# Decoder trunk on one core: values as stationary weights, key blocks merged by the mask, gelu in one function, last sums earlier

## The chip, the cores and the metric

The kernel runs on one core of a Trainium2 chip. A time is the device time of one execution in microseconds (us), and a kernel's time is the median of its runs. TensorE is called PE here, VectorE DVE, ScalarE ACT, GpSimd POOL and SyncE SP, as the profile does; PEld is PE's loading of stationary weights.

## The reference

Two layers work on 256 positions of width 2048 in float32. What matters here:

```python
for l in range(2):
    h = rms_norm(x, mix_norm[l])
    q, k, v, uv, gate_logits = split(h @ w_in[l])      # 1024, 256, 256, 2048, 4096 columns
    q, k = rope(rms_norm(q)), rope(rms_norm(k))        # 16 query heads, 4 key heads of 64
    # query i sees the 128 keys i-127 .. i; one learned sink for each head joins the softmax
    branch_a = softmax(q k^T / 8, window, sink) @ v @ w_attn_branch[l]
    u, v2 = split(gelu(uv))                            # the tanh form of gelu
    branch_b = (u * (tril(W_s) @ layer_norm(v2) + b)) @ w_sgu_branch[l]
    g = sigmoid(gate_logits)
    x = x + (g[:, :2048] * branch_a + g[:, 2048:] * branch_b) @ w_out[l]
    h2 = rms_norm(x, ffn_norm[l])
    x = x + (silu(h2 @ w_gate[l]) * (h2 @ w_up[l])) @ w_down[l]   # width 5632
```

## The kernel before

**The weight stream.** The positions are two tiles of 128 rows, t = 0 and 1. A weight matrix is cut into chunks of 512 columns, and a chunk into raw tiles of 256 rows (128 partitions x 2 x 512, 512 KB). Each raw tile is one entry of a list that is fixed before the program is written. SP loads it (L218). ACT rounds it to a high part `whi` (L244), and DVE subtracts that to give the low part `wlo` (L245). The activations are held in the same way as `uh` and `ul`. `add_product` then makes three matmuls of 128x512 for each of 2 x 128 rows (L340, L341): high by high, low by high, high by low. An ordinary entry multiplies both position tiles, so it is 12 matmuls.

Where two chunks are multiplied by the same activations (`product_pair`), a part of them goes through a scheme of seven products instead of eight. Its entries (tags P1 to P7) have 6 matmuls each; DVE makes differences of raw tiles for them (L229), and of the activations: `sums` (L499), rounded to `sh` by ACT (L484) and `sl` by DVE (L485). After P5, ACT copies one accumulator into `kept` (L363) and moves another into its place (L364), and P6 adds to the accumulator that has been read.

`whi` and `wlo` have four buffers each. The stream loads 7 entries ahead and splits 4 ahead, so ACT can start a `whi` when PE has ended the entry four places earlier.

**What sets the order.** PE's instructions stand in the order in which the program is written. All other work hangs on a count of ticks. `step()` writes one entry; two products make a tick, so an ordinary entry is one tick and a 6-matmul entry half of one. `after(n, fn)` puts `fn` n ticks ahead, and `tick()` writes what is due. On ACT, DVE and POOL a scheduler orders the instructions at build time; SP and POOL also hold queues from which transfers start.

**Attention.** For position tile t and key head g (4 query heads), `scores` multiplies queries by all keys of one or two blocks (`psc`, L754; 128 keys at t = 0, 256 at t = 1), adds a mask on DVE (L758), takes maximum, exponentials and sums. Five ticks later `weights` transposes the 128x128 blocks on PE (`ppt`, L783): 4 at t = 0 and 8 at t = 1. Three ticks later `values` multiplies them by v (`po`, L793), with the transposed probabilities as the stationary operand and 64 columns of v as the moving one, and DVE divides by the sum (L797). For each c, a half of the query heads, the result `att` is transposed (`transposed`, L410) by DVE and by 16 small transfers on SP's queue (L416).

**Spatial gating.** `half` brings chunks of u and v out of PSUM, halved; `gelu` then takes a square and a tanh on ACT and two products on DVE for each of eight 128x512 tiles in a layer. `center`, `scaled` and `shifted` normalize v, `mix` multiplies it by the spatial matrix `wsT` (`psg`, L871). The spatial matrix is transposed on PE 40 ticks after the layer's start (`pw`, L653) into two PSUM tiles that `ppt` uses too, and DVE copies it out (L654).

**The feed-forward stage** runs in rounds of 4, 4 and 3 chunks. The activations of a round's first chunk (`hid`) get their sums at the ticks of `WINO_HID`, and the down projection needs them.

## Time and profile before

| | |
|---|---|
| median of 3 runs | 2461.22 us (2460.16 to 2461.9) |
| profiled execution, its own time | 2457.45 us |
| its span, first to last instruction | 2455.7 us |
| PE busy | 2438.1 us (99%) |
| DVE busy | 1999.5 us (81%) |
| ACT busy | 1472.5 us (60%) |
| POOL busy | 315.6 us (13%) |
| matmuls of L340 and L341 | 10398 |

A busy share is a mean over the stages. PE's matmuls are pipelined: each shows some 0.39 us, but one starts every 0.23 us, so what a matmul costs is read from the distance between starts and not from its length. In the rows, `out<-in` names the tiles, then come the shapes and the count.

### The profile page before, as it was taken

Reading aid. Unit: us, or ns where it says so; the run is one execution under the profiler, and the core shown is the slowest. Engines: PE = TensorE matmul, PEld = TensorE weight load, DVE = VectorE, ACT = ScalarE, POOL = GpSimd, SP = SyncE. Lnnn points to the kernel's source line nnn. Section 1 sums busy time; section 2 is a strip of 40 time slices with the busy share of each in tenths; the row PEclk is TensorE's granted clock in tenths of the full one; section 3 lists DMA queues with packets and bytes.
Section 4 is the critical chain, followed back from the end, with each engine's and each line's share of the span. In section 5 each row is a group of like instructions: output and inputs, shape, how many; then the busy total and the mean of one; then the engine's idle time right before and its main releaser. Section 6 shows DMA issues by size and latency. Waiting matters only on the chain.

```text
span 2455.7 us, 31363 instructions
## 1 busy us (share of the span) xinstructions
PE 2438.1 (99%) x10968; PEld 2012.6 (82%) x10968; DVE 1999.5 (81%) x2320; ACT 1472.5 (60%) x1842; POOL 315.6 (13%) x592
## 2 busy tenths in 40 slices
PE   9999999999999999999999999999999999999999
PEld 7888888888888888887887888888888888888877
DVE  6798676797978997899877986768878789978996
ACT  5567544576655665566655665545666556655664
POOL 3100002132210111001101000021322101110110
PEclk9999999999999999999999999999999999999999
DMA  9555657576667657665747446675767675667654
GB/s 299 196 187 163 212 198 220 186 236 210 220 217 233 210 176 231 230 203 170 229 155 257 152 157 223 202 215 177 246 202 236 204 245 189 200 209 241 203 179 139
DMA packets 280782, 506.74 MB, mean 206 GB/s; under 512 B 28272, under 2 KB 40144, under 8 KB 280624
## 3 DMA queue, kind: packets, MB, share of 16 engines
q1 hardware_dynamic: 262544, 486.35, 61.0%
q0 software_dynamic: 17760, 18.12, 2.8%
q8 instruction: 86, 1.41, 0.2%
q14 instruction: 72, 0.59, 0.1%
q10 hardware_dynamic: 320, 0.27, 0.0%
HBM read 475.27 MB, written 2.10 MB: 194 GB/s over the span
## 4 chain that ended last, share of the span: by engine, by line
PE 90%; DVE 3%; DMA 3%; SPq 1%; issue 1%; ACT 1%; DVEq 0%; ACTq 0%
PE acc L340 59%; PE acc L341 29%; DMA raw<-in_w_in_dram 2%; DVE wlo L245 2%; SPq L416 1%; ACT whi L244 1%; PE po L793 1%; PE psc L754 0%; PE ppt L783 0%; DVE raw L229 0%; PE psg L871 0%; PE pt L453 0%; DMA raw<-in_w_up_dram 0%; DMA raw<-in_w_down_dram 0%; DVE box L410 0%
## 5 line engine op out<-in xcount | busy, mean ns | idle before, releaser
L244 ACT ACTIVATE whi<-raw 128x1024 fp32r<-128x1024 f32 (+1 forms) x1074 | 1132.0, 1059 | 883.0 <-PE acc L341 623.4
L245 DVE TENSOR_TENSOR wlo<-raw,whi 128x1024 fp32r<-128x1024 f32 (+1 forms) x1075 | 1301.3, 1219 | 399.0 <-ACT whi L244 386.7
L340 PE MATMUL acc<-whi,uh 128*128 128x512 f32 x2994 | 1170.3, 391 | 1.2 <-ACT uh L439 1.2
L340 PE MATMUL acc<-wlo,uh 128*128 128x512 f32 x2994 | 1167.1, 390 | 3.0 <-DVE wlo L245 2.9
L341 PE MATMUL acc<-whi,ul 128*128 128x512 f32 x2994 | 1166.4, 390 | 0.0
L340 PEld LDWEIGHTS acc<-wlo,uh 128*128 128x128 f32 x2994 | 562.6, 188 | 123.2 <-DVE wlo L245 6.0
L340 PEld LDWEIGHTS acc<-whi,uh 128*128 128x128 f32 x2994 | 562.6, 188 | 117.7 <-ACT uh L439 1.4
L341 PEld LDWEIGHTS acc<-whi,ul 128*128 128x128 f32 x2994 | 562.3, 188 | 117.8 <-DVE ul L444 0.5
L416 POOL DMA_DIRECT2D tt<-box x544 | 266.5, 497 | 1697.0 <-ACT whi L244 695.5
L229 DVE TENSOR_TENSOR raw<-raw,raw 128x1024 f32<-128x1024 f32 x236 | 287.8, 1219 | 1.6 <-DMA raw<-in_w_up_dram 0.8
L341 PE MATMUL acc<-whi,sl 128*128 128x512 f32 x472 | 184.0, 390 | 3.2 <-DVE sl L485 3.2
L340 PE MATMUL acc<-whi,sh 128*128 128x512 f32 x472 | 184.8, 392 | 1.7 <-ACT acc L364 1.7
L340 PE MATMUL acc<-wlo,sh 128*128 128x512 f32 x472 | 184.2, 390 | 0.0
L341 PEld LDWEIGHTS acc<-whi,sl 128*128 128x128 f32 x472 | 88.6, 188 | 22.5 <-DVE sl L485 4.0
L340 PEld LDWEIGHTS acc<-whi,sh 128*128 128x128 f32 x472 | 88.6, 188 | 20.9 <-ACT acc L364 2.1
L340 PEld LDWEIGHTS acc<-wlo,sh 128*128 128x128 f32 x472 | 88.7, 188 | 18.0
L366 DVE TENSOR_TENSOR kept<-acc,kept 128x512 f32<-128x512 f32 x94 | 64.3, 684 | 10.1 <-PE acc L341 10.1
L369 ACT ACTIVATE acc<-kept 128x512 f32<-128x512 f32 x94 | 54.9, 586 | 4.3 <-DVE kept L366 4.2
L888 DVE SCALAR_TENSOR_TENSOR xs<-acc,xs 128x512 f32<-128x512 f32 (+1 forms) x66 | 42.0, 668 | 8.4 <-PE acc L341 8.1
L436 DVE TENSOR_TENSOR ul<-tt,uh 128x512 fp32r<-128x512 f32 x52 | 34.0, 684 | 2.9 <-ACT uh L435 2.9
L435 ACT ACTIVATE uh<-tt 128x512 fp32r<-128x512 f32 x52 | 29.8, 618 | 9.4 <-DMA tt<-box 9.4
L312 POOL TENSOR_TENSOR rv<-ve,neg_half 128x4 f32<-128x4 f32 x8 | 11.9, 1486 | 172.9 <-DVE ve L839 159.5
(137 smaller groups left out, 874.8 us busy)
## 6 DMA issues: line engine op xcount, KB each, us to landing
raw<-in_w_in_dram SPq DMA_DIRECT2D x239, 512.0 KB, 4.7
raw<-in_w_gate_dram SPq DMA_DIRECT2D x176, 512.0 KB, 4.4
raw<-in_w_up_dram SPq DMA_DIRECT2D x176, 512.0 KB, 4.9
raw<-in_w_down_dram SPq DMA_DIRECT2D x176, 512.0 KB, 5.0
raw<-in_w_out_dram SPq DMA_DIRECT2D x64, 512.0 KB, 5.0
tt<-box POOLq DMA_DIRECT2D x544, 32.0 KB, 4.2
raw<-in_w_attn_branch_dram SPq DMA_DIRECT2D x32, 512.0 KB, 5.6
raw<-in_w_sgu_branch_dram SPq DMA_DIRECT2D x32, 512.0 KB, 4.4
```

The source lines that it names most:

```text
L229: self.last = nc.vector.tensor_tensor(out=self.raws[d], in0=self.raws[x], in1=self.raws[y], op=ALU.subtract)
L244: self.high = nc.scalar.activation(hi[:, i, :], raw[:, i, :], AF.Copy)
L245: self.last = nc.vector.tensor_tensor(out=lo[:, i, :], in0=raw[:, i, :], in1=hi[:, i, :].bitcast(F32), op=ALU.subtract)
L340: nc.tensor.matmul(ps, a, part[:, kk, :], start=first and kk + n == 0, stop=False, skip_group_check=True)
L341: nc.tensor.matmul(ps, b, hi[:, kk, :], start=False, stop=kk == 1, skip_group_check=True)
L366: nc.vector.tensor_tensor(out=p.kept[:, int(tag == "P7"), :], in0=a[1], in1=p.kept[:, 1, :], op=ALU.add)
L369: nc.scalar.activation(ps, p.kept[:, t, :], AF.Copy)
L416: q.dma_start(dst[j * B:(j + 1) * B, i], box[i * B:(i + 1) * B, j])
L435: nc.scalar.activation(h, s_, AF.Copy)
L436: nc.vector.tensor_tensor(out=l, in0=s_, in1=h.bitcast(F32), op=ALU.subtract)
L793: nc.tensor.matmul(po[:, h, :], pT[kb][:, h, :], self.kv[:, kb, KVW + g * HD:KVW + (g + 1) * HD], start=kb == 0, stop=kb == t)
L888: nc.vector.scalar_tensor_tensor(out=xs[:, t, sl], in0=sums[t][:, i * w:(i + 1) * w], scalar=scale, in1=xs[:, t, sl], op0=ALU.mult, op1=AL ...
```

## The change

- **Values.** v is now the stationary operand (128 keys x 64 columns) and the transposed probabilities of four heads are the moving one (512 columns). Two key heads write to the two halves of one PSUM tile, partitions 0 to 63 and 64 to 127. The result is already transposed, so `att`, its transposing and its transfers go; ACT and DVE take `uh` and `ul` from it. Heads lie in another order, so the 32 loads of `w_attn_branch` become 64 of half the partitions (`rows_of`). The division by the sum moves to the probabilities ahead of their transposing.
- **Key blocks.** Each query sees 128 of 256 keys: for each key column, one of the two blocks. At t = 1 ACT copies the later block's scores and DVE overwrites those that the mask forbids with the earlier block's (`copy_predicated`). Exponentials, maximum and transposing run over 128 columns. `values` multiplies all of it by the earlier block's v, and the part that the `causal` mask lets through by the later v less the earlier, and adds the two; ACT copies all of it out of PSUM and DVE the masked part.
- **Ticks.** Scores, weights and values have their own tables of ticks (`SCORES`, `W_TURN`, `VALUES`); `spatial` moves from 40 to 34.
- **gelu** is the ACT function `Gelu_apprx_tanh`, four tiles at a time: one ACT instruction in place of two, and no DVE products. It and Exp need different tables on ACT.
- **Sums.** In the last round the sums come at the ticks of `WINO_END`; in the others the first two steps of `WINO_HID` come later; some transposing of `hid` moves by a few ticks or to both queues.

Over the program, ACT gets 14 table loads where it had 4; PE has 64 transposes `ppt` where it had 96, and 24 matmuls `po` of 512 columns where it had 96 of 64 (the profile shows two records for each of these `po` matmuls, and one for a `ppt`).

PE's queue in layer 0, where the first values are made. `pw` is the spatial matrix, `acc` the ordinary products. Before:

```order
L653 MATMUL pw_1283<-ident,wsraw_804 128x128 x4
L653 MATMUL pw_1289<-ident,wsraw_917 128x128 x4
L793 MATMUL po_1295<-kv_471,pT_1223 128x64 x4
L340 MATMUL acc_1313<-whi_1229,uh_140 128x512
L340 MATMUL acc_1313<-wlo_1230,uh_140 128x512
L341 MATMUL acc_1313<-whi_1229,ul_141 128x512
```

After, for the first two key heads at once:

```order
L351 MATMUL acc_1296<-wlo_1452,uh_348 128x512
L352 MATMUL acc_1296<-whi_1451,ul_349 128x512
L821 MATMUL po_1539<-pT_1309,kv_471 64x512 x2
L351 MATMUL acc_1387<-wlo_1496,sh_807 128x512
L351 MATMUL acc_1387<-whi_1495,sh_807 128x512
```

One key head took four matmuls of 64 columns, one for each of its four query heads, and the next key head four more, later in the queue. Now two key heads take one matmul of 512 columns each, side by side in the queue. The spatial matrix no longer stands right ahead of them: it moved to tick 34 and comes some rows earlier.

ACT's queue in layer 1, in the stage that takes u. `pr` are exponentials, `es` the sink's, `u` and `sq` belong to gelu. Before:

```order
L771 ACTIVATE pr_12562,den_12578<-pr_12562,negm_12573 128x256 x4
L768 ACTIVATE es_12575<-es_12575 128x4
L244 ACTIVATE whi_12663<-raw_12600 128x1024
L811 ACTIVATE u_12679<-acc_12230,rhalf_2070_10713 128x512
L818 ACTIVATE sq_12682<-u_12679 128x512
L811 ACTIVATE u_12679<-acc_12231,rhalf_2073_10720 128x512
L244 ACTIVATE whi_12687<-raw_12542 128x1024
L821 ACTIVATE sq_12682<-sq_12682 128x512
L244 ACTIVATE whi_12722<-raw_12628 128x1024
L785 ACTIVATE pT_12708<-ppt_12703 128x512
L785 ACTIVATE pT_12715<-ppt_12710 128x512
L818 ACTIVATE sq_12717<-u_12679 128x512
```

After, with `whi_12449` just ahead of these rows and a `whi_12498` just behind them:

```order
L791 ACTIVATE pr_12369,den_12387<-pr_12369,negm_12382 128x128 x4
L849 ACT_TABLE_LOAD
L849 ACTIVATE u_12259<-u_12259 128x512
L824 ACTIVATE uh_12436<-po_12438 128x4x128
L849 ACTIVATE u_12259<-u_12259 128x512
L787 ACT_TABLE_LOAD
L787 ACTIVATE es_12384<-es_12384 128x4
L255 ACTIVATE whi_12468<-raw_12316 128x1024
L840 ACTIVATE u_12465<-acc_12001,rstd_2041_10596 128x512
L840 ACTIVATE u_12465<-acc_12002,rstd_2044_10603 128x512
L849 ACT_TABLE_LOAD
L849 ACTIVATE u_12465<-u_12465 128x512
```

In these rows three table loads stand now, and one `whi` where there were three.

DVE's queue in layer 0 at the end of the last feed-forward round. The products that use `sl` are those of `whi_9917` before and of `whi_9806` after. Before:

```order
L245 TENSOR_TENSOR wlo_9918<-raw_9806,whi_9917 128x1024
L245 TENSOR_TENSOR wlo_9928<-raw_9877,whi_9927 128x1024
L499 TENSOR_TENSOR sums_9896<-flat_9643,sums_9896 128x256
L245 TENSOR_TENSOR wlo_9947<-raw_9899,whi_9946 128x1024
L229 TENSOR_TENSOR raw_9806<-raw_9903,raw_9806 128x1024
L485 TENSOR_TENSOR sl_9941<-sums_9896,sh_9940 128x1024
L245 TENSOR_TENSOR wlo_9967<-raw_9806,whi_9966 128x1024
```

After:

```order
L256 TENSOR_TENSOR wlo_9752<-raw_9397,whi_9751 128x1024
L256 TENSOR_TENSOR wlo_9774<-raw_9719,whi_9773 128x1024
L496 TENSOR_TENSOR sl_9699<-sums_9659,sh_9698 128x1024
L240 TENSOR_TENSOR raw_9719<-raw_9721,raw_9719 128x1024
L256 TENSOR_TENSOR wlo_9797<-raw_9733,whi_9796 128x1024
L256 TENSOR_TENSOR wlo_9807<-raw_9719,whi_9806 128x1024
L256 TENSOR_TENSOR wlo_9817<-raw_9771,whi_9816 128x1024
```

`sl` stood behind the `wlo` of the product that needs it, and behind three more instructions; now it stands three instructions ahead of that product's `wlo_9807`.

The diff, cut to its core:

```diff
...
-WINO_HID = 7, 8, 17, 18, 19, 20
+WINO_HID = 11, 12, 17, 18, 19, 20
+WINO_END = 9, 10, 12, 13, 14, 15
...
-Q_FIRST = 17
-Q_STEP = 5
+W_TURN = 9
+SCORES = (17, 22, 27, 32), (37, 42, 47, 52)
+V_GELU, V_STEP = 4, 5
+U_GELU, U_MIX = 2, (3, 9)
+VALUES = (34, 44), (54, 64)
 LOAD_BY = (2, 4, 5, 5)
 FIRST_PART = [[(("kv", 0),), (("q", 0),)] + early + [(("v", 0),), (("v", 1),), (("gate", 1), ("u", 0)), (("u", 1), ("gate", 2)),
                                                   (("gate", 3), ("gate", 4))]
               for early in ([(("q", 1),), (("gate", 0),)], [(("q", 1), ("gate", 0))])]
...
     def single(key, w):
 
         return Plan(key, [], [half(w, h, "X") for h in range(w.shape[0] // (2 * P))])
+
+    def rows_of(raw, w, h):
+
+        if w.shape[0] != QW or not any(w is a for a in by_heads):
+            return [(raw, w[2 * h * P:2 * (h + 1) * P, :].rearrange("(k p) n -> p k n", p=P))]
+        rows = w.rearrange("(c a k d) n -> c a d k n", c=2, a=2, d=HD)
+        k = 2 * (h % 2)
+        return [(raw[a * HD:(a + 1) * HD], rows[h // 2, a, :, k:k + 2]) for a in range(2)]
 
...
-                        self.loaded = nc.sync.dma_start(raw, src)
-                    else:
-                        for i in range(2):
-                            self.loaded = nc.sync.dma_start(raw[:, i:i + 1], src[:, i:i + 1])
+                    for dst, src in rows_of(raw, w, h):
+                        if self.raws:
+                            self.loaded = nc.sync.dma_start(dst, src)
+                        else:
+                            for i in range(2):
+                                self.loaded = nc.sync.dma_start(dst[:, i:i + 1], src[:, i:i + 1])
                     self.raws[key] = raw
                 self.asked += 1
...
         for n, i in ((13, 2), (17, 3), (21, 0), (25, 1)):
             after(n, lambda i=i: pl.fetch(i))
-        after(40, pl.spatial)
+        after(34, pl.spatial)
 
...
+            if c == 0:
+                self.base = slot_no[0]
+            gone = slot_no[0] - self.base
             for t in range(NT):
-                for g in (2 * c, 2 * c + 1):
-                    after(n, lambda t=t, g=g: self.scores(t, g))
-                    n += Q_STEP
-            after(n + 6, lambda: transposed(self.attT, c, self.att[c], queue=nc.sync))
+                for i in range(2):
+                    after(SCORES[c][2 * t + i] - gone, lambda t=t, g=2 * c + i: self.scores(t, g))
+                after(VALUES[c][t] - gone, lambda t=t: self.values(t, c))
 
         def turn_queries(self, c, q):
             tt = slot([P, 4, 4, NT, B], name="tt")
...
                                      start=True, stop=True)
-                nc.vector.tensor_tensor(out=pr[:, :, j, :nk], in0=pscore[:, :, :nk],
-                                        in1=mk.unsqueeze(1).to_broadcast([P, 2, nk]), op=ALU.add)
-            pr4 = pr.rearrange("p i j k -> p (i j) k")
+                mk = mask.unsqueeze(1).to_broadcast([P, 2, P])
+                if t == 0:
+                    nc.vector.tensor_tensor(out=pr[:, :, j, :], in0=pscore[:, :, :P], in1=mk, op=ALU.add)
+                else:
+                    nc.scalar.activation(pr[:, :, j, :], pscore[:, :, P:], AF.Copy)
+                    nc.vector.copy_predicated(pr[:, :, j, :], mk.bitcast(mybir.dt.uint32), pscore[:, :, :P])
             mx = tiny(4, "mx")
...
-        def weights(self, t, g, pr4, rd):
-            pT = []
-            for kb in range(t + 1):
-                pt = ps_tr.tile([P, 4, P], F32, tag="tr", name=nm("ppt"))
-                for h in range(4):
-                    nc.tensor.transpose(pt[:, h, :], pr4[:, h, kb * P:(kb + 1) * P], ident)
-                pT_ = temp((P, 4, P), "pT")
-                nc.scalar.activation(pT_, pt, AF.Copy)
-                pT.append(pT_)
...
+            after(W_TURN, lambda: self.weights(t, g, pr4))
+
+        def weights(self, t, g, pr4):
+            if g % 2 == 0:
+                self.pT[t, g // 2] = [slot([P, 2, 4, P], name="pT") for _ in range(t + 1)]
+            pT = self.pT[t, g // 2]
+            pt = ps_tr.tile([P, 4, P], F32, tag="tr", name=nm("ppt"))
             for h in range(4):
-                for kb in range(t + 1):
-                    nc.tensor.matmul(po[:, h, :], pT[kb][:, h, :],
-                                     self.kv[:, kb, KVW + g * HD:KVW + (g + 1) * HD],
-                                     start=kb == 0, stop=kb == t)
-            o = (g % 2) * 256
-            nc.vector.tensor_tensor(out=self.att[g // 2][:, t, o:o + 256].rearrange("p (h d) -> p h d", d=HD),
-                                    in0=po, in1=rd.unsqueeze(2).to_broadcast([P, 4, HD]), op=ALU.mult)
+                nc.tensor.transpose(pt[:, h, :], pr4[:, h, :], ident)
+            nc.scalar.activation(pT[0][:, g % 2], pt, AF.Copy)
+            if t == 1:
+                nc.vector.tensor_tensor(out=pT[1][:, g % 2], in0=pt, in1=causal.unsqueeze(1).to_broadcast([P, 4, P]),
+                                        op=ALU.mult)
+
+        def values(self, t, c):
+            if t == 0:
+                self.out[c] = slot([P, 4, S], F32R, "uh"), slot([P, 4, S], F32R, "ul")
+            units = self.out[c]
+            po = ps_at.tile([P, 4, P], F32, tag="at", name=nm("po"))
+            pT = self.pT[t, c]
+            for k in range(t + 1):
+                for a in range(2):
+                    v = (1 - k) * KVW + (2 * c + a) * HD
+                    nc.tensor.matmul(po[a * HD:(a + 1) * HD], self.kv[:, 0, v:v + HD], pT[k][:, a],
+                                     start=k == 0, stop=k == t)
+            uh, ul = (x[:, :, t * P:(t + 1) * P] for x in units)
+            nc.scalar.activation(uh, po, AF.Copy)
+            nc.vector.tensor_tensor(out=ul, in0=po, in1=uh.bitcast(F32), op=ALU.subtract)
+            if t == NT - 1:
+                self.attT[c] = units
 
     class Spatial:
 
 
         def __init__(self, pl, nrm):
             self.pl, self.nrm = pl, nrm
-            self.vt, self.sguT = [None] * 2, [None] * 2
+            self.vt, self.ut, self.sguT = [None] * 2, [None] * 2, [None] * 2
 
         def half(self, ps, name):
 
             dst = slot([P, NT, CW], name=name)
             for t in range(NT):
-                nc.scalar.activation(dst[:, t, :], ps[t], AF.Copy, scale=self.nrm.rh[t])
+                nc.scalar.activation(dst[:, t, :], ps[t], AF.Copy, scale=self.nrm.r[t])
             return dst
 
-        def gelu(self, dst, t):
-
-            xh = dst[:, t, :]
-            sq = temp(name="sq")
-            nc.scalar.activation(sq, xh, AF.Square, scale=2.0)
-            nc.vector.scalar_tensor_tensor(out=sq, in0=sq, scalar=1.0 / GELU_A, in1=xh,
-                                           op0=ALU.add, op1=ALU.mult)
-            nc.scalar.activation(sq, sq, AF.Tanh, scale=2.0 * GELU_C * GELU_A)
-            nc.vector.scalar_tensor_tensor(out=xh, in0=sq, scalar=1.0, in1=xh, op0=ALU.add, op1=ALU.mult)
+        def gelu(self, both):
+
+            last = self.att.exps
+            for dst in both:
+                for t in range(NT):
+                    with tc.issue_after(last.ins):
+                        last = nc.scalar.activation(dst[:, t, :], dst[:, t, :], AF.Gelu_apprx_tanh)
+            self.att.exps = last
 
         def v(self, c, ps):
...
+            after(V_GELU, lambda: self.gelu(self.vt))
+            for i in range(4):
+                after(V_GELU + 1 + V_STEP * i, lambda i=i: self.center(i // 2, i % 2))
 
         def center(self, c, t):
...
+                pe, soon = c == len(hT) - 1 == 2, c == 3 or c == 1 and len(hT) == 3
                 after(3 if pe else 1 if soon else 2,
-                      lambda: transposed(hT, c, hid, on_pe=pe, wino=WINO_HID if c == WINO else None,
-                                         queue=None if soon else nc.gpsimd, late=-2 if soon else 0))
+                      lambda: transposed(hT, c, hid, on_pe=pe, wino=None if c != WINO else WINO_HID if len(hT) == 4 else WINO_END,
+                                         queue=None if soon else nc.gpsimd, late=-2 if c == 3 else 4 if c == 1 and len(hT) == 4 else 2 if c == 2 else 0))
 
```

70 lines of the change are left out of this document (35 added, 35 removed).

## The prediction

> **What bounds the kernel now.** I read the page's totals and the shares by engine of the chain that ended last, then stretches of the timeline, then the waits and the groups by form.
>
> ```profile
> span 2455.7 us, 31363 instructions
> PE 2438.1 (99%) x10968; PEld 2012.6 (82%) x10968; DVE 1999.5 (81%) x2320; ACT 1472.5 (60%) x1842; POOL 315.6 (13%) x592
> PE 90%; DVE 3%; DMA 3%; SPq 1%; issue 1%; ACT 1%; DVEq 0%; ACTq 0%
> 600.01 0.39 PE L340 MATMUL acc<-whi,uh 128*128 128x512 f32 x1
> 600.24 0.39 PE L340 MATMUL acc<-wlo,uh 128*128 128x512 f32 x1
> ```
>
> PE is busy all but 17.6 us of the span and is 90% of the chain. The last two rows (start, duration) are ordinary products: one starts 0.23 us after the other (0.227 over longer stretches), so the 10398 of them are about 2360 us, and the change leaves them as they are. What it can win is the rest of PE's time: attention's own matmuls, and waits. DVE and ACT have room on the whole, so work taken from them counts only where PE waits for it.
>
> **Values.** In PE's timeline, four stretches around the matmuls in question:
>
> ```profile
> 126.45 1.00 PE L793 MATMUL po<-kv,pT 128*128 128x64 f32 x8
> 127.27 0.48 PE L340 MATMUL acc<-whi,uh 128*128 128x512 f32 x1
> 127.58 0.39 PE L340 MATMUL acc<-wlo,uh 128*128 128x512 f32 x1
> ...
> 160.72 1.89 PE L793 MATMUL po<-kv,pT 128*128 128x64 f32 x16
> 162.57 0.50 PE L340 MATMUL acc<-wlo,uh 128*128 128x512 f32 x1
> 162.91 0.39 PE L340 MATMUL acc<-whi,uh 128*128 128x512 f32 x1
> ...
> 249.93 1.02 PE L871 MATMUL psg<-v,wsT 128*128 128x256 f32 x4
> 250.60 0.58 PE L340 MATMUL acc<-whi,uh 128*128 128x512 f32 x1
> 251.02 0.40 PE L340 MATMUL acc<-wlo,uh 128*128 128x512 f32 x1
> ...
> 132.93 1.14 PE L754 MATMUL psc<-kT,qT 64*128 64x256 f32 x8
> 134.00 0.66 PE L783 MATMUL ppt<-ident,pr 128*128 128x128 f32 x4
> L793 PE MATMUL po<-kv,pT 128*128 128x64 f32 x192 | 23.1, 270 | 0.0
> ```
>
> Eight `po` records take 0.82 us to the next start, and the product after them starts its neighbour 0.31 later instead of 0.23: 0.90. Sixteen take 1.85 + 0.11 = 1.96. The 192 records are eight stretches of each kind: 8 x 0.90 + 8 x 1.96 = 22.9 us. All of it is PE's own time, so all of it is on the path.
>
> After, 24 matmuls of 512 columns, two records each. Their price is not in the trace; the nearest row is `psg`, four records of 256 columns in 0.67 + 0.19 = 0.86, so 0.215 for 256 columns, 0.43 for 512, and 0.86 for a matmul. Each pair goes to two halves of the output columns. Whether halves run side by side is shown for rows only: `psc` uses half of PE's rows, its eight records of 256 columns would be 1.72 one after another, and took 1.07, which is 0.86 for four pairs and 0.2 at the edges. Taken so, t = 0 is one pair, 0.86 + 0.2, and t = 1 two pairs, 1.72 + 0.2; four of each (two halves of heads, two layers) are 11.9. I take that: **-11.0**. The bounds: one after another, 4 x (1.72 + 3.44 + 0.4) = 22.2, a gain of only 0.7; and side by side without edges, a gain of 12.6.
>
> **Transposes.**
>
> ```profile
> 150.24 1.09 PE L783 MATMUL ppt<-ident,pr 128*128 128x128 f32 x8
> 151.08 0.47 PE L340 MATMUL acc<-whi,sh 128*128 128x512 f32 x1
> ```
>
> Eight `ppt` are 0.84, four 0.43. There are 16 fours instead of 24: **-3.4**. But less of this work stands together: between products PE's queue has 61 stretches of other work where it had 55, at some 0.09 each for the edge (above): **+0.5**.
>
> **Waits that go.** From the waits of PE (us in all, times, the longest), and from the windows and the timeline behind one of them (the granted clock of the window is its third figure from the end, 0.66):
>
> ```profile
> PE acc L341 <- DVE sl L485: 3.2, 2, 1.6
> PE acc L340 <- DVE wlo L245: 2.9, 5, 0.8
> PE ppt L783 <- DVE wsT L654: 2.4, 1, 2.4
> PE acc L340 <- ACT acc L364: 1.7, 1, 1.7
> PE psc L754 <- DVE att L797: 0.7, 1, 0.7
> 1345.00:1350.00 5.00, 4.97 (x17) 4.02 (x18) 5.00 (x8) 1.84 (x4) 0.00 (x0) 0.66 0.64 233
> 1346.50 0.63 PE L340 MATMUL acc<-whi,uh 128*128 128x512 f32 x1
> 1346.93 0.63 PE L340 MATMUL acc<-wlo,uh 128*128 128x512 f32 x1
> ```
>
> - `ppt` waits 2.4 for a PSUM tile that the spatial matrix holds, since `spatial` came just ahead of it at tick 40. At 34 no `ppt` is near. Behind this wait the granted clock is 0.66 for some microseconds, and eight products start 0.43 apart instead of 0.23, 1.6 more. Both go: **-4.0**. The matrix must be there six ticks sooner:
>
> ```profile
> wsraw<-in_w_spatial_dram SPq DMA_DIRECT2D x4, 256.0 KB, 9.1
> ```
>
>   its four loads are asked for at ticks 13 to 25 and land in 9.1 us; from 25 to 34 are nine ticks of 12 x 0.227 us, 24 us. Nothing is late.
> - `psc` waits for `att`, which goes: **-0.7**.
> - `sl` (3.2, once a layer in the last round) stood behind the `wlo` of its own product, and now stands ahead of it. The wait for L364 (1.7) is of the same place, in layer 1: **-4.9**. What is late next is ACT's copy there:
>
> ```profile
> 2383.05 0.57 ACT L363 ACTIVATE kept<-acc 128x512 f32<-128x512 f32 x1
> 2383.76 1.06 ACT L244 ACTIVATE whi<-raw 128x1024 fp32r<-128x1024 f32 x1
> 2384.73 0.58 ACT L364 ACTIVATE acc<-acc 128x512 f32<-128x512 f32 x1
> 2385.36 0.50 PE L340 MATMUL acc<-whi,sh 128*128 128x512 f32 x1 [1.68 <-ACT acc L364]
> ```
>
>   The copy stands behind a `whi` that cannot start until PE frees its buffer. In the new order ACT has two `whi`, two `uh`, two `hid`, `kept` and this copy there, 5.4 to 5.9 us, under the 24 products (5.4 us) that PE has ahead. I take 0.3 in each layer: **+0.6**; it lies between 0 and the old 3.2 + 1.7.
>
> **gelu and its tables.** Tanh and Exp shared a table here; the built program now has 14 loads for 4.
>
> ```profile
> 1326.85 1.06 ACT L244 ACTIVATE whi<-raw 128x1024 fp32r<-128x1024 f32 x1 [0.29 <-DMA raw<-in_w_in_dram]
> 1327.92 1.28 ACT L771 ACT_TABLE_LOAD   x1
> L771 ACT ACTIVATE pr<-pr,negm 128x128 f32<-128x128 f32 x32 | 12.4, 390 | 4.5 <-DVE negm L764 4.5
> L821 ACT ACTIVATE sq<-sq 128x512 f32<-128x512 f32 x16 | 9.8, 619 | 1.5 <-DVE sq L819 1.5
> L244 ACT ACTIVATE whi<-raw 128x1024 fp32r<-128x1024 f32 x1071 | 1130.2, 1060 | 883.0 <-PE acc L341 623.4 <-DVE raw L229 123.9 <-issue 47.5
> L245 DVE TENSOR_TENSOR wlo<-raw,whi 128x1024 fp32r<-128x1024 f32 x1071 | 1298.7, 1221 | 399.0 <-ACT whi L244 386.7 <-DMA raw<-in_w_up_dram 3.0
> L819 DVE SCALAR_TENSOR_TENSOR sq<-sq,u 128x512 f32<-128x512 f32 x8 | 5.5, 686 | 2.6 <-ACT sq L818 2.6
> ```
>
> A load is 1.28, and starts 0.01 behind the instruction ahead of it. Ten more are 12.8 us of ACT. Against them 16 gelu instructions go (9.8), and the copies added and taken away are about even. ACT idles 883 us ahead of `whi`, 623 of it waiting for PE, so the sum costs nothing; a burst does, where it delays a `whi` by more than PE's lead. The worst is layer 1's u stage, the rows shown with the change: from `whi_12449` to `whi_12498` and its `wlo` are three `whi` (3.2), four exponentials (1.6), three loads (3.8), three gelus, a `uh` and two copies (3.8), `es` (0.2) and the `wlo` (1.2): 13.8, less some tenths where ACT's instructions overlap. PE has 48 products and half a microsecond of small work ahead of that entry: 11.4. The wait lies between 0 and 2.4; with layer 0's burst about covered I take **+1.5**.
>
> The Trainium skill speaks against this part: "ScalarE: Activation LUTs", in "What ACT_TABLE_LOAD costs", gives 1283 ns for the load and about 1380 ns of drain, and its "Rules for kernel authors" say to do all of one table set before switching. By that page the burst would be 4.1 us longer and the sum -16 instead of -20. The trace shows the load with that length and no drain ahead of it.
>
> DVE loses 32 gelu products (0.69 each, 22 us), transposes and `att`, and gains 16 predicated copies and 24 products: about 25 us less. It is credited nothing, since `wlo` already waits 387 us for `whi`. New couplings (DVE's predicated copy waits for ACT's copy; `ppt` for the division ahead of it, due five ticks sooner) have slack by the table of ticks; a miss costs between nothing and one `wlo` (1.2) each, and there are two or three kinds. For these small waits I take **+1.0** (0 to 3).
>
> **Loads.**
>
> ```profile
> raw<-in_w_attn_branch_dram SPq DMA_DIRECT2D x32, 512.0 KB, 5.6
> ```
>
> They become 64 of half the partitions. The stream asks seven entries ahead, 7 x 12 x 0.227 = 19 us; a load would have to take over three times as long to be seen. SP loses 64 small transfers of `att`, takes 16 of `hid` from POOL, and gains the 32 loads, so its queue is shorter. I take nothing; by the same bound, nothing is lost below a landing of 19 us.
>
> **The sum.** -11.0 - 3.4 + 0.5 - 4.0 - 0.7 - 4.9 + 0.6 + 1.5 + 1.0 = -20.4 on a profiled execution of 2457.45 (span 2455.7), 3.8 below the median shown, 2461.22. I set the difference against the median: **2440.8 us**.
>
> **The rivals.** 0.2%, 4.9 us, is about what a measurement of this kernel can tell from no change.
> - *Pairs in strict order.* If a matmul starts only with or after the one written ahead of it, the four records of t = 0 take three slots of 0.43 instead of two, and t = 1 five instead of four: 4 x (1.29 + 2.15 + 0.4) = 15.4, 3.5 more: **2444.3**. Against it: `psc` is written two matmuls for one half of the rows, then two for the other, and in that order could not have paired as its 1.07 us shows. The Trainium skill has this rule: "TensorE: Matmul & The Clock Gate", in "Part 3: Packing small matmuls — row/col tiling", says matmuls start and end in program order.
> - *No packing.* The two `po` of a pair both take their moving operand through all 128 rows, where `psc`'s two halves have 64 rows each; so they may run one after the other, the bound above, a gain of 0.7. **2451.1**; this part of the change would then do nothing. Nothing in the trace excludes it.
> - *The last round waits as before.* ACT's copy, or a late `sums`, takes the place of `sl`: 4.9 is not won, 0.6 is in it. **About 2445.1**. For it: that stage has both engines near full; against it: `sl` is now three instructions earlier.
> - *Slower.* The table loads fall where PE's lead is gone. For it: PE waits for `wlo` five times even now (2.9 in all, above). By the durations above, the v stage's burst of two loads and four gelus is 5.0, the u stage's of three loads, four gelus and four exponentials 7.9, in layer 1 with a `uh`, two copies and `es` 10.0. If nothing of them is covered, PE waits 27.9, and behind each of the four waits the clock drops, 1.6 each as at 1345: 34.3 us. 2461.2 - 21.9 (the sum without its 1.5) + 34.3 = **2474**. It decides once 27 of the 34 show. Against it: ACT's idle time, and each burst has about four entries' lead.
>
> **How the numbers follow.** The forecast has 0.56 (2440.8; its own range 2436 to 2446), strict order 0.13, no packing 0.12, the last round 0.07, slower 0.12. The low end is the sum without its 3.1 of allowances and with the edgeless pairs, 2436, rounded down to 2435; the high end takes in no packing with its burst and small waits at their upper bounds, 2451 + 3, and part of the way to the slow case, 2457. Faster are the first four cases, less 0.05 for a no packing that meets the upper bounds and part of the bursts: 0.83; same is that 0.05; slower the last, 0.12.
>
> **What would show it.** In the profile after: `po` as 48 records, a pair of halves 0.43 apart from the next and not 0.86; its eight stretches 12 us in sum. No wait of `ppt` for `wsT`, of `psc` for `att`, of L341's successor for `sl`; no window of clock 0.66. Table loads of 1.28 with at most 2 us of PE waiting for a `wlo` near 1432 and 200 to 240; more than 5 there makes the prediction wrong on its first count, `po` stretches of 1.9 and 3.6 on its second.

## The result and the profile after

| | before | after |
|---|---|---|
| median | 2460.99 us (2460.16 to 2461.9) | 2436.02 us (2434.74 to 2437.63) |
| profiled execution | 2457.45 us | 2435.76 us |
| its span | 2455.7 us | 2434.1 us |

The ratio of the times is 0.9899, with a 95% interval of 0.9883 to 0.9915: 25.0 us less between the medians, where 20.2 was forecast (2440.8); the time is 1 us above 2435, the low end of the forecast. The two spans lie only 21.6 apart; where the other 3.4 us come from is a question of its own below.

The totals and the chain's shares of the page after:

```profile
span 2434.1 us, 30977 instructions
PE 2423.8 (100%) x10792; PEld 1989.7 (82%) x10792; DVE 1976.2 (81%) x2290; ACT 1470.4 (60%) x1844; POOL 307.6 (13%) x577
PE 94%; DVE 2%; DMA 2%; ACT 1%; SPq 1%; issue 1%; DVEq 0%; ACTq 0%
```

PE was the bound and still is; its idle time fell from 17.6 to 10.3 us, and its busy time by 14.3. DVE lost 23 us, where the working had about 25, and ACT lost 2, where it had about 3 more.

The values, in PE's timeline after, t = 0 and t = 1:

```profile
153.10 0.39 PE L352 MATMUL acc<-whi,ul 128*128 128x512 f32 x1
153.42 1.08 PE L821 MATMUL po<-pT,kv 128*64 128x512 f32 x4
154.43 0.50 PE L351 MATMUL acc<-wlo,sh 128*128 128x512 f32 x1
154.77 0.39 PE L351 MATMUL acc<-whi,sh 128*128 128x512 f32 x1
...
184.27 0.39 PE L352 MATMUL acc<-whi,ul 128*128 128x512 f32 x1
184.59 1.94 PE L821 MATMUL po<-pT,kv 128*64 128x512 f32 x8
186.46 0.50 PE L351 MATMUL acc<-whi,uh 128*128 128x512 f32 x1
186.80 0.40 PE L351 MATMUL acc<-wlo,uh 128*128 128x512 f32 x1
```

Four records of 512 columns take 1.01 us to the next start, eight take 1.87. At 0.43 a record, one after another, they would take some 1.7 and 3.4, so pairs run side by side. With the edges on both sides (0.09 ahead, 0.11 behind) that is 1.21 and 2.07.

PE's waits after (the longest four groups), and the place of the second of them in PE's and ACT's timelines:

```profile
PE acc L351 <- DVE wlo L256: 2.2, 4, 0.8
PE acc L351 <- ACT u L840: 1.5, 1, 1.5
PE pwarm L302 <- DVE warm L297: 1.1, 1, 1.1
PE acc L351 <- ACT uh L450: 0.9, 1, 0.9
```

```profile
1437.13 0.18 ACT L791 ACTIVATION_READ_ACCUMULATOR pr<-pr,negm 128x1 f32 x1
1437.32 1.28 ACT L849 ACT_TABLE_LOAD   x1
1438.61 0.63 ACT L849 ACTIVATE u<-u 128x512 f32<-128x512 f32 x1
1439.15 0.58 ACT L824 ACTIVATE uh<-po 128x512 fp32r<-128x512 f32 x1
1439.63 0.62 ACT L849 ACTIVATE u<-u 128x512 f32<-128x512 f32 x1
1440.27 1.28 ACT L787 ACT_TABLE_LOAD   x1
1441.56 0.21 ACT L787 ACTIVATE es<-es 128x4 f32<-128x4 f32 x1
1441.67 1.04 ACT L255 ACTIVATE whi<-raw 128x1024 fp32r<-128x1024 f32 x1
1442.62 1.25 ACT L840 ACTIVATE u<-acc,rstd 128x512 f32<-128x512 f32 x2
...
1441.20 0.60 PE L806 MATMUL ppt<-ident,pr 128*128 128x128 f32 x4
1443.34 0.50 PE L351 MATMUL acc<-whi,uh 128*128 128x512 f32 x1 [1.54 <-ACT u L840]
```

The waits for `sl`, for ACT's copy in the last round, for `wsT` and for `att` are gone. New is one wait of 1.5 for ACT's copies of u out of PSUM: they stand behind two table loads, two gelus, a `uh`, an `es` and a `whi`.

PE's time in the two profiled executions by what it went to (the distance between starts; for work between products, with its edges, less the products' own 0.227):

| | before | after | difference | the sum had |
|---|---|---|---|---|
| values | 21.7 | 13.1 | -8.6 | -11.0 |
| scores, transposes, mixing, spatial matrix, without waits | 36.5 | 33.8 | -2.7 | -3.4 + 0.5 |
| waits for `sl` and ACT's copy, last round | 5.3 | 0 | -5.3 | -4.9 + 0.6 |
| wait for `wsT` and the clock drop behind it | 4.0 | 0 | -4.0 | -4.0 |
| wait for `att` | 0.7 | 0 | -0.7 | -0.7 |
| waits near 122 and 1322 | 1.7 | 0.5 | -1.2 | 0 |
| wait for the copies of u | 0 | 1.5 | +1.5 | +1.5 |
| late load near 306 | 0 | 0.8 | +0.8 | 0 |
| small waits of new couplings | 0 | 0 | 0 | +1.0 |
| the rest, in small pieces | | | -1.4 | 0 |

### The profile page after: what moved, and what is told of

Its sections match the earlier page's. It is cut to its first block, busy times and chain, and to the rows that moved or that the text cites. A ratio compares the mean times of both kernels' runs of the same rounds, so it can differ in the third digit from the quotient of the medians.

```text
span 2434.1 us, 30977 instructions
## 1 busy us (share of the span) xinstructions
PE 2423.8 (100%) x10792; PEld 1989.7 (82%) x10792; DVE 1976.2 (81%) x2290; ACT 1470.4 (60%) x1844; POOL 307.6 (13%) x577
## 3 DMA queue, kind: packets, MB, share of 16 engines
q8 instruction: 84, 1.38, 0.2%
## 4 chain that ended last, share of the span: by engine, by line
PE 94%; DVE 2%; DMA 2%; ACT 1%; SPq 1%; issue 1%; DVEq 0%; ACTq 0%
PE acc L351 62%; PE acc L352 31%; DMA raw<-in_w_in_dram 1%; DVE wlo L256 1%; PE psc L769 0%; DMA raw<-in_w_attn_branch_dram 0%; SPq L427 0%; ACT whi L255 0%; PE po L821 0%; PE pt L464 0%; DVE raw L240 0%; PE psg L903 0%; PE ppt L806 0%; DVE ul L455 0%; SPq L229 0%
## 5 line engine op out<-in xcount | busy, mean ns | idle before, releaser
L427 POOL DMA_DIRECT2D tt<-box x528 | 258.6, 497 | 1650.3 <-ACT whi L255 537.3
L377 DVE TENSOR_TENSOR kept<-acc,kept 128x512 f32<-128x512 f32 x94 | 64.4, 685 | 10.2 <-PE acc L352 10.2
L1014 ACT ACTIVATE hid<-acc,rstd 128x512 f32<-128x512 f32 x44 | 28.6, 681 | 6.4 <-PE acc L352 6.3
```

The source lines that it names most:

```text
L377: nc.vector.tensor_tensor(out=p.kept[:, int(tag == "P7"), :], in0=a[1], in1=p.kept[:, 1, :], op=ALU.add)
L427: q.dma_start(dst[j * B:(j + 1) * B, i], box[i * B:(i + 1) * B, j])
L1014: nc.scalar.activation(hid[:, t, :], g[t], AF.Silu, scale=norm.r[t])
```

## The experiments

The theory: three parts, of which each is read off PE's queue: cheaper values (they run in pairs), waits that go because work was moved, and one burst of table loads that shows. The rivals: no pairs, or pairs in strict order; waits that go only because DVE and ACT have less to do; table loads dearer or cheaper than the waits show. No run has the key blocks alone: what the scores and transposes gain, 2.7, is read from the two profiles.

**The kernel before, profiled again**

> The kernel before, unchanged, profiled once more. The medians moved 25.0 us but the two profiled spans only 21.6. Theory: executions of the kernel before differ among themselves, by waits that the clock's drops lengthen, and the profiled one was a short one; a second profile then shows a span nearer 2459, with a wait or a stretch of lower clock that the first had not, and a median of 2461. Rival: the profiling itself takes some 3 us off this kernel, and the second profile is 2455 to 2456 again.

Measured: a span of 2460.6 us, and a median of 2459.95 (ratio to before 1.0001, 0.9993 to 1.001). The same wait for `sl` near the end, in PE's timeline of the first profile of before:

```profile
2375.06 0.40 PE L340 MATMUL acc<-wlo,sh 128*128 128x512 f32 x1
2377.03 0.50 PE L341 MATMUL acc<-whi,sl 128*128 128x512 f32 x1 [1.58 <-DVE sl L485]
2377.37 0.39 PE L340 MATMUL acc<-whi,sh 128*128 128x512 f32 x1
```

In the second profile:

```profile
2378.36 0.40 PE L340 MATMUL acc<-wlo,sh 128*128 128x512 f32 x1
2380.34 0.61 PE L341 MATMUL acc<-whi,sl 128*128 128x512 f32 x1 [1.58 <-DVE sl L485]
2380.75 0.63 PE L340 MATMUL acc<-whi,sh 128*128 128x512 f32 x1
2381.17 0.63 PE L340 MATMUL acc<-wlo,sh 128*128 128x512 f32 x1
```

And the window behind it (the granted clock is the third figure from the end, 0.66):

```profile
2380.00:2385.00 5.00, 4.66 (x13) 3.68 (x14) 3.10 (x4) 1.35 (x2) 0.00 (x0) 0.66 0.27 98
```

The wait is the same 1.58. Behind it products start 0.23 apart in the one execution, and eight of them 0.43 apart in the other, 1.6 us more. The same profile has eleven such products behind the wait for `wsT`, which is 3.1 long here. So a long wait costs more than itself in some executions, by chance, and the first profile of before was a short one by luck. The other executions point the same way. The 38 executions of before that ran beside the experiments have their mean granted clock on record: the span is 2460.8 us in the mean of three at 0.997, 2458.1 for seventeen at 0.998, 2456.2 for sixteen at 0.999 and 2453.3 for two at 1.000. The theory holds: the profiling takes nothing off.

**Only the spatial matrix moved**

```diff
--- before
-        after(40, pl.spatial)
+        after(34, pl.spatial)
```

> The kernel before with the spatial matrix at tick 34 alone. Theory: the wait of the transposes for it (2.4) and the clock drop behind it (1.6) go, and the 1.0 us of PE work now standing ahead of the late loads near 122 and 1322 covers those two waits (0.7 and 1.0): 5.7 us less than before, 2455. Rival: only the wait and the drop go, 4.0 less, and the waits at 122 and 1322 stay. Rival: the transposes wait for another late tile there, and nothing is won.

Measured: 2454.6 us beside 2459.71 for before on the same chip, ratio 0.9983 (0.9974 to 0.9992), so 5.1 less. The wait for `wsT` is gone and so is its clock drop. Near 122 nothing is left, near 1325 0.4 of the 1.0. But this profile has new waits in the v and u stages, 1.2 and 1.0 near 1371 and 1375, and the wait for ACT's copy in the last round is absent, which this edit does not touch directly. The theory's main part holds by the trace, and the one near 1325 in part; the sum meets the time through two other things that about cancel. The time alone can't tell the theory's 5.7 from the first rival's 4.0: the interval of the ratio runs from 2.0 to 6.4 us less.

**Only the sums' ticks**

```diff
--- before
-WINO_HID = 7, 8, 17, 18, 19, 20
+WINO_HID = 11, 12, 17, 18, 19, 20
+WINO_END = 9, 10, 12, 13, 14, 15
...
-                pe, soon = c == len(hT) - 1 == 2, c == 3
+                pe, soon = c == len(hT) - 1 == 2, c == 3 or c == 1 and len(hT) == 3
...
-                      lambda: transposed(hT, c, hid, on_pe=pe, wino=WINO_HID if c == WINO else None,
-                                         queue=None if soon else nc.gpsimd, late=-2 if soon else 0))
+                      lambda: transposed(hT, c, hid, on_pe=pe, wino=None if c != WINO else WINO_HID if len(hT) == 4 else WINO_END,
+                                         queue=None if soon else nc.gpsimd, late=-2 if c == 3 else 4 if c == 1 and len(hT) == 4 else 2 if c == 2 else 0))
```

> The kernel before with the ticks of the sums and of the transposing of the feed-forward activations as after, alone. Theory: the two waits for sl (3.2) and the one for ACT's copy in the last round (1.7) go, with nothing in their place: 4.9 to 5.4 us less, 2456. Rival: ACT's copy is late next, 0.3 in each layer: 4.3 less. Rival: the waits go only because gelu and attention took work from DVE, and here they come back elsewhere: under 2 less.

Measured: 2451.62, ratio 0.9967 (0.9955 to 0.998): 8.1 less, against 4.9 to 5.4. Of PE's waits in this profile the longest now is the one that this edit leaves alone:

```profile
PE ppt L784 <- DVE wsT L655: 3.1, 1, 3.1
PE acc L341 <- DVE wlo L246: 2.1, 4, 0.8
```

No `sl` and no copy of the last round: the waits go without any help from gelu or attention, so the third expectation falls, and with ACT's copy not late either, the second. The surplus of about 3 us could be clock drops behind these three waits in executions of before, but that is not shown: of its two profiles one has a drop behind one of the three. That a drop is chance shows here too. Behind the wait of 3.1, which ended at 1343.9, the granted clock stayed at 1.00 (third figure from the end):

```profile
1345.00:1350.00 5.00, 5.00 (x24) 4.10 (x23) 5.00 (x7) 3.43 (x6) 0.00 (x0) 1.00 0.38 140
```

**The sums' ticks undone in the changed kernel.** The same diff the other way round.

> The changed kernel with the ticks of the sums and of the transposing of the feed-forward activations as before. Theory: the two waits of 2.0 for sl and the one of 2.1 for ACT's copy come back, with a clock drop of 1.6 behind one or two of the three: 6 to 9 more than the changed kernel, 2442 to 2445, as the kernel before lost 8.1 by the same edit. Rival: only the waits themselves count, 4.9 more, 2440.5. Rival: with work taken from DVE sl is in time anyway: no change.

Measured: 2443.42, ratio to before 0.9939 (0.9927 to 0.9952), 7.4 to 7.8 more than the changed kernel's two medians, which were taken in other batches. Of PE's waits:

```profile
PE acc L351 <- DVE sl L495: 3.2, 2, 1.6
...
PE acc L350 <- ACT whi L254: 1.7, 1, 1.7
PE acc L350 <- ACT acc L374: 1.7, 1, 1.7
```

Both old waits are back at their old size, so they had not gone because DVE had less to do. The row for `whi` is another matter: it comes late near 306, where the half loads are. By the distance between starts the old waits are 5.3 in this profile, with no stretch of half clock behind any of them, and the late loads 2.9, where the changed kernel has 0.8. So the time lies in the theory's range, but this profile does not show the theory's reason for what goes beyond 5.3.

**Both moves in the kernel before**

> The kernel before with both edits that only move work: the spatial matrix at tick 34 and the ticks of the sums. Theory (the waits and PE's own work are two separate parts of the gain): 8.1 and 5.1 add to 12 to 13 less than before, 2447, and what is left to the changed kernel, 11 to 12, is PE's time for values and transposes. Rival: the two moves meet in the same wait of the last round, and give 9 together, 2451.

Measured: 2450.21 (its runs from 2446.91 to 2453.44) beside 2458.5, ratio 0.9965 (0.9952 to 0.9977): 8.3 less, not 12 to 13. That is the rival's number, but not for the rival's reason, since the two waits for `sl`, the one for ACT's copy and the one for `wsT` are all gone. In their place the profiled execution has a late load at 29.6 (2.1, with a stretch of half clock behind it), and the waits near 1371 that the spatial move brought alone. Whether the two moves add in the kernel before stays open.

**The changed kernel again**

> The changed kernel once more, as the base for its variants on this chip: 2436, a ratio of 0.990, with the waits of 1.5 near 1443 and 0.6 near 306 in its profile again. Rival: these two are chance, and another profile has them elsewhere or not at all.

Measured: 2435.67, ratio 0.9902 (0.9887 to 0.9917). The wait for the copies of u is 1.5 again; the one near 306 is 0.3 this time. The first comes again in the same program, the second depends on when a load lands.

**Values without pairs**

```diff
--- after
-            po = ps_at.tile([P, 4, P], F32, tag="at", name=nm("po"))
...
-            for k in range(t + 1):
-                for a in range(2):
+            uh, ul = (x[:, :, t * P:(t + 1) * P] for x in units)
+            po = [ps_at.tile([P, 4, P], F32, tag="at", name=nm("po")) for a in range(2)]
+            for a in range(2):
+                for k in range(t + 1):
...
-                    nc.tensor.matmul(po[a * HD:(a + 1) * HD], self.kv[:, 0, v:v + HD], pT[k][:, a],
+                    nc.tensor.matmul(po[a][:HD], self.kv[:, 0, v:v + HD], pT[k][:, a],
...
+            for a in range(2):
+                h = slice(a * HD, (a + 1) * HD)
+                nc.scalar.activation(uh[h], po[a][:HD], AF.Copy)
+                nc.vector.tensor_tensor(out=ul[h], in0=po[a][:HD], in1=uh[h].bitcast(F32), op=ALU.subtract)
```

The order of the two loops changes here as well; the next experiment does that alone.

> The changed kernel with the two values matmuls of a pair written to two PSUM tiles, both on partitions 0 to 63, so that both use the same half of PE's columns; ACT and DVE take them out in two pieces each. Theory (the halves run side by side in the changed kernel): a pair costs 0.86 more and there are twelve, so 10.3 us more than the changed kernel, 2446, with po stretches of 1.9 and 3.6 us. Rival: the halves never ran side by side and the stretches of 1.0 and 1.9 are cheap records: no change, 2436. Rival: the two further pieces on ACT and DVE cost more than the matmuls, a wait on uh or ul of over 1 us near 155 or 1470.

Measured: 2445.56, ratio to before 0.9946 (0.9932 to 0.996): 9.9 more than the changed kernel. PE's timeline at t = 1:

```profile
185.29 0.39 PE L352 MATMUL acc<-whi,ul 128*128 128x512 f32 x1
185.61 3.65 PE L822 MATMUL po<-pT,kv 128*64 128x512 f32 x8
189.19 0.50 PE L351 MATMUL acc<-whi,uh 128*128 128x512 f32 x1
```

3.58 instead of 1.87: the eight records now run one after another. At t = 0 it is 1.86 instead of 1.01, so the eight stretches cost 10.2 more, the theory's size. The 9.9 is the sum of more than that: this profile has a wait of 0.7 for `ul` near 255, under the last expectation's 1 us, and the wait of 1.5 for the copies of u is absent, since ACT's instructions come in another order in this build. Without the pairs the new form of the values would cost some 23.3, more than the old one's 21.7: the pairs carry all of its gain.

**Values in another order**

```diff
--- after
-            for k in range(t + 1):
-                for a in range(2):
+            for a in range(2):
+                for k in range(t + 1):
```

> The changed kernel with the values matmuls of t = 1 written in another order: both of the one half of the columns, then both of the other. If matmuls start in the order in which they are written, the second half starts with the last record of the first, seven slots of 0.43 instead of four, 1.3 us more in each of four stretches: 5.2 more, 2441. If each half of the columns is served for itself, the stretch stays 1.9 and the time 2436.

Measured: 2435.19, ratio 0.9907 (0.9893 to 0.9921): no change. PE's timeline:

```profile
184.01 1.94 PE L821 MATMUL po<-pT,kv 128*64 128x512 f32 x8
185.88 0.50 PE L351 MATMUL acc<-whi,uh 128*128 128x512 f32 x1
```

1.87 again. All four records of the one half are written first, and yet the records start in twos, the first two 14 ns apart. Two records of the same half can't be such a pair, since they start 0.43 apart in the run without pairs. So each half of the columns is served for itself. The strict order of the Trainium skill ("TensorE: Matmul & The Clock Gate", "Part 3: Packing small matmuls — row/col tiling") is not what these records show.

**Whole loads for the attention branch**

```diff
--- after
-        by_heads += cols_of(w_attn_branch[l], NCH)
-        plans += [single(("att", l), w) for w in by_heads[-NCH:]]
+        plans += [single(("att", l), w) for w in cols_of(w_attn_branch[l], NCH)]
...
-            for k in range(t + 1):
-                for a in range(2):
+            for a in range(2):
+                for k in range(t + 1):
...
-                    nc.tensor.matmul(po[a * HD:(a + 1) * HD], self.kv[:, 0, v:v + HD], pT[k][:, a],
-                                     start=k == 0, stop=k == t)
+                    for j in range(2):
+                        nc.tensor.matmul(po[j * HD:(j + 1) * HD, 2 * a:2 * a + 2], self.kv[:, 0, v:v + HD],
+                                         pT[k][:, a].rearrange("p (i j) q -> p j i q", j=2)[:, j],
+                                         start=k == 0, stop=k == t)
```

> The changed kernel with the heads laid out in pairs of neighbours, so that the attention branch's weights are loaded in 32 whole transfers of 512 KB and 128 partitions as before; the values matmuls become twice as many of 256 columns. Theory (transfers to half the partitions move at half the rate and leave the stream short near 306): ACT's waits for these loads and PE's 0.3 to 0.8 near 306 go, landing is 5 to 6 us again; the matmuls cost the same by columns, so 0.3 to 0.8 less than the changed kernel, 2435. Rival: the wait near 306 comes from the sixteen small transfers ahead of the loads on SP's queue, and stays. Rival: smaller matmuls cost 0.1 more each at their edges, up to 2 more in all.

Measured: 2436.13, ratio 0.9908 (0.9894 to 0.9922): no difference in the time. The changed kernel's window from 300 to 305 (the last figures are the granted clock, the DMA engines' busy share and GB/s), and this one's:

```profile
300.00:305.00 5.00, 5.00 (x23) 4.10 (x22) 1.83 (x2) 1.50 (x2) 0.00 (x0) 1.00 1.03 227
```

```profile
300.00:305.00 5.00, 5.00 (x24) 4.08 (x23) 2.32 (x3) 2.45 (x3) 0.00 (x0) 1.00 1.02 345
```

ACT's waits for these loads (us in all, times, the longest), in the changed kernel and here:

```profile
ACT whi L255 <- DMA raw<-in_w_attn_branch_dram: 21.0, 13, 2.8
```

```profile
ACT whi L254 <- DMA raw<-in_w_attn_branch_dram: 6.2, 8, 1.8
```

With the DMA engines busy all the time, transfers to 64 partitions moved 227 GB/s and transfers to 128 moved 345; a half load lands in 8.0 us, a whole one here in 4.8. So the rate is shown, and ACT's waits follow from it. The values, now twice as many matmuls of 256 columns, take 1.01 and 1.88 to the next start, so the last expectation falls. The sixteen small transfers ahead of these loads on SP's queue are not enough by themselves: they hold the queue for 10 us in the changed kernel and for 11 here, and here PE does not wait. PE's wait near 306 is in six of the seven profiles with half loads, 0.3 to 0.6 of idle time in most (in the one without pairs it comes near 312) and 1.7 in the one with the sums' old ticks; it is not in the one with the other order. In neither profile with whole loads is it there. What it is worth is not seen in the time, and this run can't isolate it. The wait of 1.5 for the copies of u is absent here as well, because ACT's order differs in this build, and against both stand a late load of another matrix near 1317 (0.8) and a stretch of half clock near 10 us.

**Gelu of u behind the copies**

```diff
--- after
-                nc.scalar.activation(dst[:, t, :], ps[t], AF.Copy, scale=self.nrm.r[t])
+                self.copied = nc.scalar.activation(dst[:, t, :], ps[t], AF.Copy, scale=self.nrm.r[t])
...
             self.ut[c] = self.half(ps, "u")
             if c == 0:
                 return
+            self.att.exps = self.copied
```

> The changed kernel with ACT's gelu of u held behind the copies of the second u chunk: its four tiles then come in one run, 10 table loads instead of 14, and the copies that PE waits for near 1443 stand ahead of the loads. Theory (that wait of 1.5 is the burst of table loads and gelus in front of the copies): it goes, 1.5 less than the changed kernel, 2434.3. Rival: the later gelu comes too late for the spatial products or delays another entry, and a wait of 1 to 2 us is back elsewhere: 2436.

Measured: 2433.44 (2433.22 to 2434.7), ratio 0.99 (0.9885 to 0.9916). PE waits for no copy of u any more. In ACT's timeline they stand ahead of a single table load:

```profile
1438.39 0.69 ACT L840 ACTIVATE u<-acc,rstd 128x512 f32<-128x512 f32 x1 [0.21 <-PE acc L352]
1438.98 1.05 ACT L255 ACTIVATE whi<-raw 128x1024 fp32r<-128x1024 f32 x1
1440.05 1.28 ACT L849 ACT_TABLE_LOAD   x1
1441.34 2.19 ACT L849 ACTIVATE u<-u 128x512 f32<-128x512 f32 x4
```

The wait of 1.5 was the burst, and it goes with it: 1.8 to 2.7 less than the medians of the kernels run beside it that keep the changed kernel's values in pairs. The intervals of the ratios overlap, so the time alone would not settle it. The trace shows that the wait goes when the copies stand ahead of the loads; how much of the time is due to it stays open, since the run with whole loads lacks the wait too and is no faster.

**Both of these edits**

> The changed kernel with both edits: gelu of u behind the copies of the second u chunk, and whole transfers for the attention branch. Theory: 1.5 for the first and up to 0.8 for the second, 2433 to 2434. Rival: the second gives nothing that a time shows, since a late load of another matrix took its place near 1317: 2434 as with the first alone.

Measured: 2433.81 (2432.78 to 2434.81), ratio 0.9899 (0.9885 to 0.9912). As the rival had it, the second edit adds nothing that a time shows. Either of the two has the lowest medians here, some 2 us below the changed kernel's, with intervals that overlap its own.

**Gelu in two functions, at the new ticks**

```diff
--- after
-                nc.scalar.activation(dst[:, t, :], ps[t], AF.Copy, scale=self.nrm.r[t])
+                nc.scalar.activation(dst[:, t, :], ps[t], AF.Copy, scale=self.nrm.rh[t])
...
+                    xh = dst[:, t, :]
+                    sq = temp(name="sq")
...
-                        last = nc.scalar.activation(dst[:, t, :], dst[:, t, :], AF.Gelu_apprx_tanh)
+                        last = nc.scalar.activation(sq, xh, AF.Square, scale=2.0)
+                    nc.vector.scalar_tensor_tensor(out=sq, in0=sq, scalar=1.0 / GELU_A, in1=xh,
+                                                   op0=ALU.add, op1=ALU.mult)
+                    with tc.issue_after(last.ins):
+                        last = nc.scalar.activation(sq, sq, AF.Tanh, scale=2.0 * GELU_C * GELU_A)
+                    nc.vector.scalar_tensor_tensor(out=xh, in0=sq, scalar=1.0, in1=xh, op0=ALU.add, op1=ALU.mult)
```

> The changed kernel with gelu by square and tanh on ACT and two products on DVE as before, at the new ticks and in the same batches: 4 table loads. Theory (the loads cost only the wait of 1.5 near 1443, and the products on DVE were covered): 2434 to 2436, that wait gone or smaller, ten loads fewer. Rival: the 22 us of products on DVE make PE wait for wlo in the u and v stages, 2 to 6 more than the changed kernel, 2438 to 2442. Rival: table loads cost more than the waits show, over 3 less, under 2433.

Measured: 2437.7, ratio 0.9914 (0.99 to 0.9927): some 2 more than the changed kernel's medians, between the theory and the first rival; the intervals overlap. Two of PE's waits:

```profile
PE ppt L810 <- DVE pr L800: 1.6, 1, 1.6
PE acc L355 <- ACT whi L259: 1.3, 2, 1.1
```

The window from 190 to 215 here, and in the changed kernel (the third figure with a count is DVE's busy time):

```profile
190.00:215.00 25.00, 23.21 (x106) 18.00 (x106) 24.12 (x52) 18.33 (x36) 2.49 (x2) 1.00 0.54 165
```

```profile
190.00:215.00 25.00, 24.91 (x118) 19.55 (x117) 23.43 (x52) 19.07 (x37) 2.01 (x2) 1.00 0.60 191
```

The wait for the copies of u is gone, as the theory had it. One of 1.6 for a DVE product stands near 210 in its place, where DVE is busy 24.1 of 25 us: the division of the probabilities, ahead of their transposing, comes late. So by this profile DVE's gelu products are not covered at the new ticks. Two late half loads near 306 and 310 (0.8 each) are in it too. The third expectation falls.

## Why the prediction was right

- **The bound.** Right: the gain is in PE's work and waits. DVE's 23 us less count only as far as they keep PE from waiting, as the run with the old gelu shows.
- **Values, -11.0.** The mechanism is right: pairs run side by side on halves of the columns as on halves of the rows. The run without pairs gives 9.9 back and the one in the other order changes nothing, so both rivals on this point fall. The size was too large by 2.4. Half of it is the price before: the quoted stretch of sixteen took 1.96, but the mean of the eight is 1.82. The other half is the edge: 0.35 for a stretch, not 0.2.
- **Transposes, -3.4, and stretches, +0.5.** Right; -2.7 with the scores and the mixing.
- **`wsT`, -4.0, and `att`, -0.7.** Right by the trace. What the step left out: the spatial matrix is 1.0 us of PE's work, and at tick 34 it stands ahead of the late loads near 122 and 1322. Their waits, 1.7 together, are 0.5 after.
- **The last round, -4.9 + 0.6.** The waits went, with nothing in their place. The 0.6 for ACT's copy is not there, in the profile after or in the run with the sums' ticks alone. That run shows that the move does it without help from the rest, and it gains more than the sum has for it, 8.1 in place of 4.3.
- **The tables, +1.5.** Place and cause are right, the waiter is not, and that the size agrees is luck, since it was worked out for the waiter that did not wait. The step named `whi_12498` and its `wlo`; PE waited for ACT's copies of u, which hold the PSUM tile that the next product needs. No drain stands ahead of this load: an exponential's sum is read out until 1437.31, the load starts at 1437.32. With the further 1.38 for each load of the Trainium skill ("ScalarE: Activation LUTs", "What ACT_TABLE_LOAD costs"), the two loads ahead of the copies would have made the wait 4.3 instead of 1.5, by an estimate. Of the bursts that the rival of a slower kernel adds up to 27.9 us, this wait of 1.5 is what shows.
- **DVE credited nothing.** For the kernel before no PE wait names a gelu product, but no run has the new gelu there. At the new ticks it is not so: the run with the old gelu has the wait of 1.6.
- **Small waits, +1.0.** None of the named kind is in the profile after. A late load of 0.8, which the step on loads put at nothing, stands in their place by chance.
- **Loads, nothing.** A half load lands in 8.0, below the bound of 19 us, and yet PE waits near 306. The step looked at one load's time to land. The rate fell to 227 GB/s, and the stream takes some 193 (512 KB in 12 x 0.227 us), so little is left to catch up with after the 10 us in which SP's queue has only small transfers.
- **The sum against one profile.** The terms came to -20.4 where the two spans differ by 21.6, through errors that about cancel (values and small waits against the rest). The medians differ by 25.0. What fits is that the waits were taken at the length of one execution: a stretch of half clock follows long waits in some executions and not in others. The profile of before had one such stretch, its second profile two, and before's clock goes with its spans, as above; after, three of four executions have a clock of 1.000. That all 3.4 come from this is not shown.

## What to carry to other kernels

Price a wait of two microseconds on PE at more than itself, and read it in two profiles before a sum is built on one. A matmul that fills half of PE's columns cost half here, its edges aside, with another for the other half beside it, in either order. When work is moved in an engine's queue, look at what it now stands in front of: 1 us of PE's work ahead of a late load was about free here, and a table load ahead of the copies out of PSUM was not.

## What the runs showed of the hardware that was not expected

The stretch of half clock lasts eight products of 0.427 us, 3.4 us, or eleven. It followed a wait of 1.6 us in one execution and not in another, and waits of 2.4 and 3.1 us in the two profiles of before, but not the wait of 3.1 in the run with the sums' ticks alone. The Trainium skill ("TensorE: Matmul & The Clock Gate", "Why this matters for your kernels") says to have no idle gap over about 3 us; the stretch began here behind less. The wait of 1.5 for the copies of u had no such stretch behind it in any of the four profiles that have it.

Transfers into 64 partitions kept the DMA engines as busy as transfers into 128 (1.03 and 1.02 of their time) and moved two thirds as much.
